# Feed-forward by seven products: weights prepared two parts ahead, sums made one unit earlier, another product order, and one halved down block instead of two

## The chip, the cores and the metric

The kernel runs on one core of a Trainium2 chip. The metric is the time of one execution on the device in microseconds (us). The kernel before has a median of 1240.38 us over three timed runs (1239.95 to 1240.4). One further execution was taken with the hardware profiler; all durations below are from it.

The core has five engines that run side by side, each in its own order: TensorE (PE: matmuls, with PEld for the loading of their weights), VectorE (DVE), ScalarE (ACT), GpSimd (POOL) and SyncE (SP, which only issues transfers). They wait for one another through semaphores. Transfers (DMA) are issued by SP, POOL and ACT, each with a queue of its own.

## The reference

One layer of an encoder: 512 tokens, 1024 features, float32. Two token mixers (a gated DeltaNet with 8 heads and a banded attention with 16) are merged; then come a cross-attention into 256 memory tokens, a SwiGLU feed-forward network (FFN) with 2816 hidden features, and a final norm. What the change touches, with its surroundings:

```python
oa = _gated_deltanet(qa, ka, va, alpha, beta, a_log[l], dt_bias[l])
oa = rmsnorm(oa, head_norm[l]) * jax.nn.silu(za.reshape(b, s, A_HEADS, A_DV))
...
x = x + _memory_xattn(rmsnorm(x, norm_xattn[l]), rmsnorm(mem, norm_mem[l]),
                      w_mq[l], w_mkv[l], w_mo[l])
gate, up = _split_cols(rmsnorm(x, norm_ffn[l]) @ w_gate_up[l], (D_FF, D_FF))
x = x + (jax.nn.silu(gate) * up) @ w_down[l]
return rmsnorm(x, norm_final)
```

## The kernel before

**Products.** Activations lie with features on the 128 partitions and tokens along the row. A float32 product is made from halves: every operand is split into a high part (`whi`, `fh`, `guh`, written by ScalarE, L111) and a low part (`wlo`, `fl`, `gul`, the rest, written by VectorE, L113), and three matmuls (high x high, high x low, low x high) are summed in PSUM. So each weight is loaded by SP into a `raw` buffer, split, and used; `raw`, `whi` and `wlo` have three buffers each.

**Order of the work.** PE runs in the order of the program text. `drive` (L173) takes the steps of the present products; after each step `advance` (L168) moves every generator in the list `pending` one step on, so `wait(n)` holds something back by n steps. A `side` generator advances once a step. ACT, DVE, POOL and SP run in an order that a scheduler of the compiler chooses; where a tile needs a buffer, the pool's ring decides whose last reader it waits for.

**Last head of the DeltaNet.** `head_out` (L494) computes `zs`, the normed and gated output of a head; `oa_tile` (L537) transposes it on PE (`oaT`, L542), one head later in general. For the last head there is no later one: it waits 6 steps and is transposed between the tiles `nat` of the next product. A `nat` tile is 24 matmuls, two k to a step.

**FFN, blocks 0 to 2.** The 22 blocks of 128 hidden features have one gate and one up product each. For the first three, `ffn_gemm` makes them plainly, each 24 matmuls of 512 tokens, on the activations before the norm; `ffn_after` (L1101) empties the gate's PSUM into `fa` (L1104: times the row factor of the norm, silu, times the factor again) and then the up product into `gu` (L1108). PSUM for these has three slots (`PM`), so the third up block takes the slot of the second gate block. Tiles `fa` have tag "c", with three buffers.

**Sums of the activations.** Beside these blocks `ffn_sums` (L1114) normalises the activations (`xn`, two tiles in each of four rounds) and makes from their quarters (feature half by token half) the seven operands of a fast 2x2 product: three plain (11, 21, 22) and four sums (T1 to T4, `ft`), each split into `fh` and `fl`, 256 tokens wide.

**FFN, units 3 to 21.** A `unit` (L1166) makes both gate and up of one block from seven products instead of eight. Its weights are the quarters of `w_g[j]` and `w_u[j]`: three plain ones (a11, a12, a22) and four sums s1 to s4 (`fs`). s1 and s3 are summed by the transfer itself: a load by SP (L1172), then an accumulating transfer by POOL (L1173, L1174). s2 and s4 are added on VectorE (L1196, L1197). `quarter` (L1156) splits one into high and low, and is called as an argument of `product` (12 matmuls of 256 tokens, L1186 to L1188), so right ahead of its use. The order is 11, T2, T1, T3, 21, T4, 22. After each product a few operations add its PSUM into `fe`, `fU`, `fW`, `fcc`; the last one (L1219) makes the block's `gu`. s1, s3 and s4 share tag "ti" with four buffers, s2 has "th".

**Down product.** `gu_split` splits a `gu` block into `guh` and `gul`. Blocks 0 to 4 are split beside units 9 to 13; of the rest, three are split ahead of the first down block and the others beside it. Of the 8 output blocks of 128 features, 0 to 5 run whole (`series`: 66 matmuls of 512 tokens, then the residual sum and the sum of squares `acc`, by POOL). Blocks 6 and 7 run in two halves of 256 tokens (`wd_last`), so that `final` (L1267), the norm of a half, can begin on the first half under the second. Its sum of squares takes `acc` and one `sq` for each halved block.

Of the kernel before, what the change touches and what calls it, by code (L numbers as in the profile page):

```python
# [40 lines left out]
def hybrid_block(  # L41
# [452 lines left out]
    def head_out(hd):  # L494

        on, ss = kT[hd], SM("ss", 4)
        pu_, pq = PD("oU"), PS("oS")
        for n in range(NT):
            c = slice(n * P, (n + 1) * P)
            nc.tensor.matmul(out=pu_[:, c], lhsT=PT[hd][:, c], rhs=vs[hd][:, c], start=True, stop=True)  # L500
        yield
        for n in range(1, NT):
            c = slice(n * P, (n + 1) * P)
            nc.tensor.matmul(out=pq[:, c], lhsT=qT[hd][:, c], rhs=S[hd, n - 1], start=True, stop=True)
        yield
# [12 lines left out]
        f = SM("f", 4)  # L518
        nc.vector.scalar_tensor_tensor(out=f, in0=ss, scalar=1.0 / P, in1=fe[hd], op0=ALU.mult, op1=ALU.add)
        nc.gpsimd.tensor_tensor(out=f, in0=f, in1=mhalf, op=ALU.pow)  # L520
        yield from wait(2)
        z = zs[hd // 2]
        zc = slice((hd % 2) * P, (hd % 2) * P + P)
        for n in range(NT):
            nc.vector.scalar_tensor_tensor(out=z[:, n, zc], in0=on[:, n * P : (n + 1) * P], scalar=f[:, n : n + 1],
                                           in1=z[:, n, zc], op0=ALU.mult, op1=ALU.mult)
# [587 lines left out]
    def ffn_sums():  # L1114

        for n in NB:
            B[n] = []
        for i in range(4):
            x = []
            for k in (i, i + 4):  # L1120
                t = TMP("xn", "th")
                nc.vector.scalar_tensor_tensor(out=t, in0=x3[k], scalar=gain(C_FFN, k), in1=stat["row3"],
                                               op0=ALU.mult, op1=ALU.mult)
# [39 lines left out]
        split(hi, lo, src)  # L1163
        return hi, lo

    def unit(j):  # L1166
        raws = [wp.tile([P, KD, P], F32, tag="raw", bufs=3, name=nm("raw")) for _ in range(2)]
        a11, a12, a22 = raws[0][:, 0:4, :], raws[0][:, 4:8, :], raws[1][:, 0:4, :]
        s1, s3, s4, s2 = (TMP("fs", t).rearrange("p (k f) -> p k f", k=4) for t in ("ti", "ti", "ti", "th"))
        nc.sync.dma_start(out=raws[0], in_=w_g[j])  # L1170
        for s in (s1, s3):
            nc.sync.dma_start(out=s, in_=w_u[j][:, 0:4, :])  # L1172
        nc.gpsimd.dma_start(out=s1, in_=w_u[j][:, 4:8, :], accum_op=ALU.add)  # L1173
        nc.gpsimd.dma_start(out=s3, in_=w_g[j][:, 0:4, :], accum_op=ALU.add)  # L1174
        nc.sync.dma_start(out=a22, in_=w_u[j][:, 4:8, :])
        e, U = TMP("fe", "c"), TMP("fU", "c")
        W, sg, cc = TMP("fW", "c"), TMP("fg", "th"), TMP("fcc", "th")
        tt = nc.vector.tensor_tensor
        rot = [PM, PD, PS, PM, PD, PM, PD]

        def product(ps, w, act):
# [8 lines left out]

        def bank(i):
            return rot[i]("fp")
        p1 = bank(0)
        yield from product(p1, quarter(a11), "11")
        nc.scalar.activation(e[:, lh], p1[:, lh], AF.Copy)
        tt(out=s2, in0=s1, in1=a11, op=ALU.add)  # L1196
        tt(out=s4, in0=a12, in1=s2, op=ALU.add)  # L1197
# [3 lines left out]
        p = bank(2)  # L1201
        yield from product(p, quarter(s1), "T1")
        tt(out=W[:, lh], in0=U[:, lh], in1=p[:, lh], op=ALU.add)
        q = bank(3)
        yield from product(q, quarter(s3), "T3")
        tt(out=U[:, rh], in0=U[:, lh], in1=q[:, lh], op=ALU.add)
        tt(out=cc[:, rh], in0=W[:, lh], in1=q[:, lh], op=ALU.add)
        p = bank(4)
        yield from product(p, quarter(a12), "21")
        tt(out=e[:, lh], in0=e[:, lh], in1=p[:, lh], op=ALU.add)  # L1210
        nc.scalar.activation(sg[:, lh], e[:, lh], AF.Silu)
        p = bank(5)
        yield from product(p, quarter(a22), "T4")
        tt(out=cc[:, lh], in0=U[:, rh], in1=p[:, lh], op=ALU.add)
        p = bank(6)
        yield from product(p, quarter(s4), "22")
        tt(out=W[:, lh], in0=W[:, lh], in1=p[:, lh], op=ALU.add)
        nc.scalar.activation(sg[:, rh], W[:, lh], AF.Silu)
# [48 lines left out]
    def final(tok, sq):  # L1267
        yield from wait(6)
        ps = [PS("r4") for _ in range(2)]
        for i, q in enumerate([acc4[:, tok]] + sq):  # L1270
            for tt in range(2):
                nc.tensor.matmul(out=ps[tt][:, 0:1], lhsT=q[:, tt * P : tt * P + P], rhs=ones[:, 0:1],  # L1272
                                 start=(i == 0), stop=(i == 2))
        var, rs = SM("r4", 2), SM("r4", 2)
        for tt in range(2):
            nc.vector.tensor_scalar(out=var[:, tt : tt + 1], in0=ps[tt][:, 0:1], scalar1=1.0 / D, scalar2=EPS,  # L1276
# [9 lines left out]
            nc.vector.tensor_tensor(out=x, in0=x, in1=pr[:, :H].unsqueeze(1).to_broadcast([P, 2, H]), op=ALU.mult)  # L1286
            (nc.scalar if i in (0, 2) else nc.sync).dma_start(out=outT[i][:, :, tok], in_=x)

    wd = series(w_d, dps, gu, wd_after, range(KD - 2), kt=KF, pieces=PIECES)
    side = gu_splits(range(5, KF))  # L1290
    for _ in range(3):
        next(side)
    drive(wd[0], side=side)
    drive(*wd[1:])
    for hf in range(2):
        tok, sq = slice(hf * H, hf * H + H), []
        drive(*[(wd_last(j, tok, PM("wd"), sq), None) for j in (KD - 2, KD - 1)])
        pending.append(final(tok, sq))
    flush()

# [71 lines left out]
```

## Time and profile before

| What | Value |
|---|---|
| median of three timed runs | 1240.38 us (1239.95 to 1240.4) |
| profiled execution | 1234.58 us, its span 1232.9 us |
| granted clock, mean over the execution | 0.989 |
| ACT, DVE, POOL busy | 47%, 62%, 12% |
| data moved | 149.28 MB, mean 121 GB/s |
| units 3 to 21 | 886.78 to 1094.51 us |
| down blocks 0 to 5 | 1094.51 to 1189.02 us |

The timed runs and the profiled execution are different executions; times inside the kernel are from the latter, and they are us from the start of the span. A row of a group or of the timeline reads "output<-inputs", with the program's names. What stands in brackets behind a row is the idle time of the engine just before it and what ended that. The granted clock is the share of TensorE's full clock that the chip's throttle let through.

### The profile page before, as it was taken

What the parts mean: (1) busy time and instruction counts of PE and PEld (TensorE: products, weight loads), DVE (VectorE), ACT (ScalarE), POOL (GpSimd) and SP (SyncE); (2) the same over time, 40 slices, a digit from 0 to 9 for tenths busy, and PEclk for the clock granted to TensorE, in tenths of its full rate; (3) what the DMA queues carried; (4) which work ended last, traced back from release to release, by engine and by line L of the source; (5) the groups of instructions that cost most, each with busy time, mean ns of one, the idle gap of its engine ahead of it and who ended that gap; (6) DMA issues with size and microseconds to landing.
All of it is one profiled execution on the core that took longest, in us unless ns stands there. A gap on an engine that the chain in (4) does not pass through costs nothing. (4 is left out here: it accounts for less than half of the span.)

```text
span 1232.9 us, 19731 instructions
## 1 busy us (share of the span) xinstructions
PE 1204.3 (98%) x7571; PEld 1052.7 (85%) x7571; DVE 764.0 (62%) x1564; ACT 584.9 (47%) x1207; POOL 144.8 (12%) x143
## 2 busy tenths in 40 slices
PE   9999999999999999999999999999899989999997
PEld 8778888899988887777888998888699989988887
DVE  5967882355633488775464654554978878882233
ACT  7573234465741477665333443443544545462232
POOL 0022230310110000000122200013011111100000
PEclk9999999999999999999999999999989999999998
DMA  7253343212433432223324462123167666743343
GB/s 278 87 177 102 123 119 98 94 43 70 149 122 106 162 103 90 90 86 111 108 98 145 135 210 83 52 69 103 49 159 184 168 159 172 190 118 94 94 124 116
DMA packets 73054, 149.28 MB, mean 121 GB/s; under 512 B 19041, under 2 KB 27649, under 8 KB 72961
## 3 DMA queue, kind: packets, MB, share of 16 engines
q1 hardware_dynamic: 66400, 137.02, 34.4%
q0 software_dynamic: 5472, 9.96, 5.1%
q8 instruction: 59, 0.97, 0.3%
q10 hardware_dynamic: 1088, 1.05, 0.2%
q14 instruction: 35, 0.28, 0.1%
HBM read 140.13 MB, written 7.88 MB: 120 GB/s over the span
## 5 line engine op out<-in xcount | busy, mean ns | idle before, releaser
L111 ACT ACTIVATE whi<-raw 128x1024 fp32r<-128x1024 f32 (+4 forms) x224 | 206.4, 926 | 310.5 <-PE g L138 80.9
L113 DVE TENSOR_TENSOR wlo<-raw,whi 128x1024 fp32r<-128x1024 f32 (+4 forms) x210 | 228.5, 1092 | 156.3 <-ACT whi L111 155.1
L1188 PE MATMUL fp<-fh,wlo 128*128 128x256 f32 x532 | 153.2, 288 | 3.7 <-DVE wlo L113 3.7
L1186 PE MATMUL fp<-fh,whi 128*128 128x256 f32 x532 | 152.8, 287 | 3.7 <-ACT whi L111 3.4
L1187 PE MATMUL fp<-fl,whi 128*128 128x256 f32 x532 | 152.6, 287 | 2.0 <-DVE fl L113 2.0
L1188 PEld LDWEIGHTS fp<-fh,wlo 128*128 128x128 f32 x532 | 104.1, 196 | 4.8 <-DVE wlo L113 4.8
L1186 PEld LDWEIGHTS fp<-fh,whi 128*128 128x128 f32 x532 | 104.1, 196 | 4.4 <-ACT whi L111 3.9
L1187 PEld LDWEIGHTS fp<-fl,whi 128*128 128x128 f32 x532 | 104.2, 196 | 2.3 <-DVE fl L113 2.2
L111 ACT ACTIVATE whi<-fs 128x512 fp32r<-128x512 f32 x76 | 46.4, 626 | 62.4 <-PE fp L1187 46.7
L203 POOL TENSOR_TENSOR acc<-acc,sq 128x512 f32<-128x512 f32 x19 | 31.6, 1665 | 265.2 <-issue 161.3
L162 PE MATMUL nat<-whi,hh 128*128 128x256 f32 x192 | 58.5, 304 | 0.4 <-DVE conv L391 0.4
L164 PE MATMUL nat<-wlo,hh 128*128 128x256 f32 x192 | 55.0, 286 | 0.0
L163 PE MATMUL nat<-whi,hl 128*128 128x256 f32 x192 | 54.9, 286 | 0.0
L113 DVE TENSOR_TENSOR wlo<-fs,whi 128x512 fp32r<-128x512 f32 x76 | 51.1, 686 | 6.0 <-ACT whi L111 5.4
L138 PE MATMUL g<-gul,whi 128*128 128x512 f32 x132 | 52.5, 398 | 1.9 <-DVE gul L113 1.9
L139 PE MATMUL g<-guh,wlo 128*128 128x512 f32 x132 | 52.2, 396 | 0.0
L137 PE MATMUL g<-guh,whi 128*128 128x512 f32 x132 | 52.0, 394 | 0.0
L799 ACT ACTIVATE P<-P,mx 128x128 f32<-128x128 f32 (+1 forms) x64 | 35.8, 560 | 28.7 <-DVE mx L797 28.5
L113 POOL TENSOR_TENSOR wlo<-raw,whi 128x1024 fp32r<-128x1024 f32 x14 | 34.0, 2430 | 106.3 <-ACT whi L111 106.3
L162 PEld LDWEIGHTS nat<-whi,hh 128*128 128x128 f32 x192 | 37.5, 195 | 1.4 <-issue 0.6
L1173 POOL DMA_DIRECT2D fs<-in_w_u x19 | 16.7, 876 | 185.5 <-DMA fs<-in_w_u 69.4
L163 PEld LDWEIGHTS nat<-whi,hl 128*128 128x128 f32 x192 | 37.4, 195 | 0.0
(416 smaller groups left out, 3327.7 us busy)
## 6 DMA issues: line engine op xcount, KB each, us to landing
raw<-in_w_g SPq DMA_DIRECT2D x22, 512.0 KB, 5.6
raw<-in_w_d SPq DMA_DIRECT2D x20, 512.0 KB, 3.6
fs<-in_w_u SPq DMA_DIRECT2D x38, 256.0 KB, 3.8
fs<-in_w_u POOLq DMA_DIRECT2D x19, 256.0 KB, 3.9
fs<-in_w_g POOLq DMA_DIRECT2D x19, 256.0 KB, 6.3
raw<-in_w_u SPq DMA_DIRECT2D x19, 256.0 KB, 4.0
raw<-in_wk SPq DMA_DIRECT2D x8, 512.0 KB, 3.8
raw<-in_wga SPq DMA_DIRECT2D x8, 512.0 KB, 3.6
```

The costliest lines, as they stand in the source:

```text
L111: nc.scalar.activation(hi, src, AF.Copy, scale=1.0 if scale is None else scale)
L113: (eng or nc.vector).tensor_tensor(out=lo, in0=src, in1=hi.bitcast(F32), op=ALU.subtract)
L137: nc.tensor.matmul(out=ps[:, :w], lhsT=hi[:, k - a, :], rhs=xh[:, n], start=first, stop=False)
L138: nc.tensor.matmul(out=ps[:, :w], lhsT=hi[:, k - a, :], rhs=xl[:, n], start=False, stop=False)
L139: nc.tensor.matmul(out=ps[:, :w], lhsT=lo[:, k - a, :], rhs=xh[:, n], start=False, stop=last)
L162: nc.tensor.matmul(out=o, lhsT=xh[:, tok], rhs=hi[:, kw, :], start=(k == 0), stop=False)
L163: nc.tensor.matmul(out=o, lhsT=xl[:, tok], rhs=hi[:, kw, :], start=False, stop=False)
L164: nc.tensor.matmul(out=o, lhsT=xh[:, tok], rhs=lo[:, kw, :], start=False, stop=(k == KD - 1))
L799: nc.scalar.activation(pr, pr, AF.Exp, scale=-1.0, bias=mx, accum_out=rs[:, t : t + 1])
L1186: nc.tensor.matmul(out=o, lhsT=hi[:, k, :], rhs=xh, start=k == 0, stop=False)
L1187: nc.tensor.matmul(out=o, lhsT=hi[:, k, :], rhs=xl, start=False, stop=False)
L1188: nc.tensor.matmul(out=o, lhsT=lo[:, k, :], rhs=xh, start=False, stop=k == 3)
```

## The change

- The last head's `oaT` waits 12 steps instead of 6.
- `ffn_sums` takes all its `fh` and `fl` buffers at the start, two operands to a tile in the pairs (11, 21), (22, T1), (T2, T3), (T4, unused). Its `xn` tiles move from tag "th" to tag "c", which they share with `fa`.
- In the units, `loads(j)` issues the transfers and the two VectorE sums of unit j. It is called within the stream of parts of the unit before, at its sixth part. `take` keeps the stream up to two parts ahead of the product that runs. s4 moves from "ti" to "th".
- The order of the products is 11, 21, 22, T2, T1, T3, T4, and the operations that empty PSUM follow it, with the same number of them.
- Blocks 5 to 12 of `gu` are split beside the last unit, 13 to 21 beside the first down block.
- Only down block 7 runs in halves; block 6 runs whole, and the final norm has one `sq` for each half.

```diff
         if hd == AH - 1:
-            yield from wait(6)
+            yield from wait(12)
             yield from oa_tile(hd)
...
+        tiles = {}
+        for at in range(4):
+            for i in range(4):
+                tiles[i, at] = [G("a" if at < 2 else "b", n, F32R) for n in ("fh", "fl")]
         for i in range(4):
             x = []
             for k in (i, i + 4):
-                t = TMP("xn", "th")
+                t = TMP("xn", "c")
...
-            his = [G("a" if i < 2 else "b", "fh", F32R) for _ in range(4)]
-            los = [G("a" if i < 2 else "b", "fl", F32R) for _ in range(4)]
             for at, n in enumerate(NB):
                 o = lh if at % 2 == 0 else rh
-                B[n].append((his[at // 2][:, o], los[at // 2][:, o]))
+                B[n].append([t[:, o] for t in tiles[i, at // 2]])
...
-    def unit(j):
+    def loads(j):
+
         raws = [wp.tile([P, KD, P], F32, tag="raw", bufs=3, name=nm("raw")) for _ in range(2)]
         a11, a12, a22 = raws[0][:, 0:4, :], raws[0][:, 4:8, :], raws[1][:, 0:4, :]
-        s1, s3, s4, s2 = (TMP("fs", t).rearrange("p (k f) -> p k f", k=4) for t in ("ti", "ti", "ti", "th"))
-        nc.sync.dma_start(out=raws[0], in_=w_g[j])
+        s1, s3, s2, s4 = (TMP("fs", t).rearrange("p (k f) -> p k f", k=4) for t in ("ti", "ti", "th", "th"))
         for s in (s1, s3):
             nc.sync.dma_start(out=s, in_=w_u[j][:, 0:4, :])
+        nc.sync.dma_start(out=raws[0], in_=w_g[j])
         nc.gpsimd.dma_start(out=s1, in_=w_u[j][:, 4:8, :], accum_op=ALU.add)
         nc.gpsimd.dma_start(out=s3, in_=w_g[j][:, 0:4, :], accum_op=ALU.add)
         nc.sync.dma_start(out=a22, in_=w_u[j][:, 4:8, :])
+        tt(out=s2, in0=s1, in1=a11, op=ALU.add)
+        tt(out=s4, in0=a12, in1=s2, op=ALU.add)
+        return a11, a12, s4, s2, s1, s3, a22
+
+    def quarters():
+        srcs = loads(NCL)
+        for j in range(NCL, KF):
+            now = srcs
+            for n in range(7):
+                if n == 5 and j + 1 < KF:
+                    srcs = loads(j + 1)
+                yield quarter(now[n])
+
+    stream, ready = quarters(), []
+
+    def take():
+        while len(ready) < 3:
+            ready.append(next(stream, None))
+        return ready.pop(0)
...
-        yield from product(p1, quarter(a11), "11")
+        yield from product(p, take(), "11")
...
-        yield from product(p, quarter(s2), "T2")
+        yield from product(p, take(), "21")
...
+        if j == KF - 2:
+            pending.append(seq(wait(10), gu_splits(range(5, 9)), wait(8), gu_splits(range(9, 13))))
...
-                                 start=(i == 0), stop=(i == 2))
+                                 start=(i == 0), stop=(i == len(sq)))
...
-    wd = series(w_d, dps, gu, wd_after, range(KD - 2), kt=KF, pieces=PIECES)
-    side = gu_splits(range(5, KF))
-    for _ in range(3):
-        next(side)
+    wd = series(w_d, dps, gu, wd_after, range(KD - 1), kt=KF, pieces=PIECES)
+    side = gu_splits(range(13, KF))
...
-        drive(*[(wd_last(j, tok, PM("wd"), sq), None) for j in (KD - 2, KD - 1)])
+        drive(*[(wd_last(j, tok, PM("wd"), sq), None) for j in (KD - 1,)])
```

Three places show how instructions move (numbers behind a name tell its buffers apart, and they differ between the two programs).

On PE at the end of the DeltaNet, before the change, the transposes of the last head follow a finished `nat` tile and stand ahead of the next:

```order
L162 MATMUL nat_3991<-whi_3790,hh_546 128x256
L163 MATMUL nat_3991<-whi_3790,hl_547 128x256
L164 MATMUL nat_3991<-wlo_3791,hh_546 128x256
L542 MATMUL oaT_4016<-ident,zs_284 128x128 x4
L162 MATMUL nat_4040<-whi_4030,hh_434 128x256
```

On PE at the same place after the change, the tile that came behind `oaT` (there `nat_4040`, here `nat_4031`) is finished first:

```order
L162 MATMUL nat_4031<-whi_4027,hh_546 128x256
L163 MATMUL nat_4031<-whi_4027,hl_547 128x256
L164 MATMUL nat_4031<-wlo_4028,hh_546 128x256
L542 MATMUL oaT_4056<-ident,zs_284 128x128 x4
L162 MATMUL nat_4068<-whi_4021,hh_434 128x256
```

So 24 matmuls moved ahead of the four transposes.

On DVE in the first FFN blocks, before the change, the second gate block's `fa` (`fa_8846`, from PSUM `ff_8678`) stands between the first and the second round's sums, 19 rows behind the first `xn`:

```order
L113 TENSOR_TENSOR fl_8646<-xn_8636,fh_8642 128x256
L113 TENSOR_TENSOR fl_8648<-ft_8650,fh_8644 128x256
L113 TENSOR_TENSOR fl_8708<-xn_8688,fh_8704 128x256
L1104 TENSOR_TENSOR fa_8846<-ff_8678,rrow_8624 128x512
L1122 SCALAR_TENSOR_TENSOR xn_8697<-x_2_6726,cst,rrow_8624 128x512
L1139 TENSOR_TENSOR ft_8712<-xn_8688 128x256
L113 TENSOR_TENSOR wlo_8883<-raw_8880,whi_8882 128x1024
```

On DVE after the change, the same `fa_8846` stands in the fourth round, 52 rows behind the first `xn`:

```order
L1149 SCALAR_TENSOR_TENSOR ft_8778<-ft_8777,xn_8765 128x256
L113 TENSOR_TENSOR fl_8652<-ft_8778,fh_8651 128x256
L113 TENSOR_TENSOR fl_8652<-ft_8777,fh_8651 128x256
L113 TENSOR_TENSOR fl_8646<-ft_8819,fh_8645 128x256
L1142 SCALAR_TENSOR_TENSOR ft_8819<-ft_8819,xn_8814 128x256
L1145 TENSOR_TENSOR ft_8820<-xn_8814,xn_8809 128x256
L1104 TENSOR_TENSOR fa_8846<-ff_8702,rrow_8624 128x512
L113 TENSOR_TENSOR fl_8638<-xn_8814,fh_8637 128x256
```

So 33 more instructions stand ahead of it, all of them sums, splits of sums, or weight splits; its buffer is one that an `xn` held (`xn_8765`, last read by the first row shown).

On SP's queue while the cross-attention's `mem_v` product runs, as one piece of the difference (`raw` from `in_w_mv` are its weights, `fs` from `in_w_u` are the loads for s1 and s3 of the units):

```order
 L120 DMA raw_7500<-in_w_mv 128x1024
-L1172 DMA fs_8918<-in_w_u 128x512
-L1172 DMA fs_8919<-in_w_u 128x512
+L1176 DMA fs_8924<-in_w_u 128x512
+L1176 DMA fs_8925<-in_w_u 128x512
+L1176 DMA fs_8996<-in_w_u 128x512
 L120 DMA raw_7506<-in_w_mv 128x1024
+L1176 DMA fs_8997<-in_w_u 128x512
 L120 DMA raw_7568<-in_w_mv 128x1024
```

The two loads of unit 3 were there already; the two of unit 4 (`fs_8996`, `fs_8997`) join them, one ahead of `raw_7506` and one ahead of `raw_7568`.

More of the change, by code (lines that the diff above doesn't have):

```diff
@@ L1192, in bank @@
             return rot[i]("fp")
[L1193 to L1199 removed]
+        p = bank(0)
+        yield from product(p, take(), "11")
+        nc.scalar.activation(e[:, lh], p[:, lh], AF.Copy)
+        p = bank(1)
+        yield from product(p, take(), "21")
+        tt(out=sg[:, lh], in0=e[:, lh], in1=p[:, lh], op=ALU.add)
+        nc.scalar.activation(sg[:, lh], sg[:, lh], AF.Silu)
+        q = bank(2)
+        yield from product(q, take(), "22")
+        p = bank(3)
+        yield from product(p, take(), "T2")
         tt(out=U[:, lh], in0=e[:, lh], in1=p[:, lh], op=ALU.add)
[L1201 to L1202 removed]
+        p = bank(4)
+        yield from product(p, take(), "T1")
         tt(out=W[:, lh], in0=U[:, lh], in1=p[:, lh], op=ALU.add)
[L1204 to L1211, printed above, removed]
[L1212 to L1213 removed]
+        tt(out=sg[:, rh], in0=W[:, lh], in1=q[:, lh], op=ALU.add)
+        nc.scalar.activation(sg[:, rh], sg[:, rh], AF.Silu)
+        p = bank(5)
+        yield from product(p, take(), "T3")
+        tt(out=U[:, rh], in0=U[:, lh], in1=p[:, lh], op=ALU.add)
+        tt(out=cc[:, rh], in0=W[:, lh], in1=p[:, lh], op=ALU.add)
+        p = bank(6)
+        yield from product(p, take(), "T4")
         tt(out=cc[:, lh], in0=U[:, rh], in1=p[:, lh], op=ALU.add)
[L1215 to L1218, printed above, removed]
         nc.vector.scalar_tensor_tensor(out=gu_tile(), in0=cc, scalar=-1.0, in1=sg, op0=ALU.mult, op1=ALU.mult)
```

3 lines of the change are left out of this document (2 added, 1 removed).

## The prediction

> **What bounds the kernel now.** I read the page's head first, for the busy shares.
>
> ```profile
> span 1232.9 us, 19731 instructions
> ...
> PE 1204.3 (98%) x7571; PEld 1052.7 (85%) x7571; DVE 764.0 (62%) x1564; ACT 584.9 (47%) x1207; POOL 144.8 (12%) x143
> ```
>
> TensorE (PE) is the bound. No matmul is saved in bulk, so a gain can only be PE's idle time and the slow matmuls behind it. Where that is, the waits of PE (us in total, times, longest) and then the windows by stage say (us, busy time and count of PE, PEld, DVE, ACT and POOL, granted clock, DMA share, GB/s).
>
> ```profile
> PE fp L1188 <- DVE wlo L113: 3.7, 4, 1.9
> PE fp L1186 <- ACT whi L111: 3.4, 2, 1.9
> PE oaT L542 <- DVE zs L525: 2.2, 1, 2.2
> PE fp L1187 <- DVE fl L113: 2.0, 1, 2.0
> PE g L138 <- DVE gul L113: 1.9, 3, 1.4
> ```
>
> ```profile
> 347.46:351.38 3.92, 1.73 (x12) 1.24 (x11) 3.02 (x6) 1.72 (x3) 1.94 (x2) 1.00 0.41 120
> 351.38:354.79 3.41, 3.41 (x19) 3.41 (x18) 1.07 (x2) 0.30 (x1) 0.00 (x0) 0.50 0.61 213
> 886.78:906.20 19.42, 14.20 (x85) 13.21 (x84) 14.84 (x34) 8.23 (x18) 2.69 (x3) 0.74 0.45 115
> 906.20:916.28 10.08, 10.08 (x86) 10.08 (x85) 8.31 (x17) 4.51 (x10) 0.86 (x1) 1.00 0.69 173
> 998.10:1013.45 15.35, 11.97 (x87) 11.56 (x85) 11.06 (x22) 7.12 (x14) 2.59 (x3) 0.89 0.60 137
> 1094.51:1113.88 19.37, 17.52 (x68) 13.29 (x67) 13.42 (x20) 9.21 (x17) 0.00 (x0) 0.91 0.38 109
> 1113.88:1128.91 15.03, 15.03 (x68) 12.39 (x66) 4.10 (x4) 4.36 (x6) 0.00 (x0) 1.00 0.34 94
> ```
>
> An undisturbed unit takes 10.08 us, an undisturbed down block 15.03. The first unit (at 886.78), unit 13 (at 998.10) and the first down block (at 1094.51) are longer, and in each the clock is below 1. A wait is thus paid twice: once idle, once in a stretch of half clock, of which the row at 351.38 is one of 3.41 us.
>
> **The change part by part.**
>
> *Last oaT, 24 matmuls later.* Here is PE around it, and VectorE's zs that it waits for.
>
> ```profile
> 347.46 0.28 PE L164 MATMUL nat<-wlo,hh 128*128 128x256 f32 x1
> 349.93 1.02 PE L542 MATMUL oaT<-ident,zs 128*128 128x128 f32 x4 [2.19 <-DVE zs L525]
> ...
> 351.59 0.41 PE L162 MATMUL nat<-whi,hh 128*128 128x256 f32 x1
> 351.80 0.41 PE L163 MATMUL nat<-whi,hl 128*128 128x256 f32 x1
> ```
>
> ```profile
> 349.43 1.14 DVE L525 SCALAR_TENSOR_TENSOR zs<-kT,f,zs 128x128 f32<-128x128 f32 x4 [0.90 <-POOL f L520]
> ```
>
> At full clock a 256-wide matmul takes 10.08/84 = 0.12 us; at half clock 0.21 (351.59 to 351.80). The half-clock stretch loses 3.41 x (1 - 0.12/0.21) = 1.5 us. With the wait: 2.2 + 1.5 = 3.7. A whole tile of 24 matmuls now stands ahead and covers 24 x 0.12 = 2.88 us: oaT's turn comes at 347.58 + 2.88 = 350.46, zs ends at 350.57. At most 0.1 stays, too short for a half-clock stretch by the row on 1.5 us below. Gain **3.7**.
>
> *First unit (19.42 - 10.08 = 9.34 us over).* Unit 3 now has its first weights split early and all four rounds of sums made beforehand, so its own stalls go. But fa and xn now share the three buffers of tag "c", and VectorE does the sums first: fa_8846, which empties the second gate block's PSUM, stood 19 rows behind the first xn and now stands 52 behind. Its durations, start to start, are in these rows:
>
> ```profile
> 861.68 1.41 DVE L1122 SCALAR_TENSOR_TENSOR xn<-x,cst,rrow 128x512 f32<-128x512 f32 x2 [1.56 <-ACT rrow L236]
> 863.01 0.68 DVE L1104 TENSOR_TENSOR fa<-ff,rrow 128x512 f32<-128x512 f32 x1
> 863.61 0.41 DVE L1139 TENSOR_TENSOR ft<-xn 128x256 f32<-128x256 f32 x1
> 863.94 0.42 DVE L113 TENSOR_TENSOR fl<-xn,fh 128x256 fp32r<-128x256 f32 x1
> ...
> 866.79 1.22 DVE L113 TENSOR_TENSOR wlo<-raw,whi 128x1024 fp32r<-128x1024 f32 x1
> 867.93 0.42 DVE L1147 SCALAR_TENSOR_TENSOR ft<-ft,xn 128x256 f32<-128x256 f32 x1
> ```
>
> ```profile
> 881.16 0.39 PE L137 MATMUL ff<-xh,whi 128*128 128x512 f32 x1
> ```
>
> One xn takes (863.01 - 861.68)/2 = 0.665 us, a 512-wide fa 0.60 (863.01 to 863.61; gu and the 512-wide wlo are taken as that), a 256-wide ft or fl 0.335 (863.61 to 863.94), a 1024-wide wlo 1.14 (866.79 to 867.93). The 52 rows are 8 xn, 37 ft and fl, 3 of fa and gu, 2 wide and 2 narrow wlo: 5.3 + 12.4 + 1.8 + 2.3 + 1.2 = 23.0 us. So fa_8846 starts at 861.68 + 23.0 = 884.7 and ends at 885.3. The third up block takes that PSUM slot and in the trace starts at 881.16: a **new wait of 4.2 us**, and about 1.6 for one half-clock stretch behind it (the 1.5 above, with room for where it falls). Queued behind that waiting matmul is all the rest of PE's work. The next slot is emptied by a gu 14 rows later: seven of 0.335 and seven of 0.60, so 885.3 + 6.6 = 891.9, while PE ends the up block at 885.3 + 5.6 + 1.6 = 892.5: not late. Unit 3 then starts 5.8 later, with bounds of 4.2 (no half clock) and 9.3 (as much as now). Gain 9.34 - 5.8 = **3.5**.
>
> [...]
>
> *Later units.* Here are the eighteen other units in one window, ScalarE's wait in them, and their transfers (KB each, median us to landing).
>
> ```profile
> 906.20:1094.51 188.31, 184.10 (x1515) 183.08 (x1513) 160.00 (x312) 96.01 (x189) 28.50 (x33) 0.99 0.67 170
> ```
>
> ```profile
> ACT whi L111 <- DMA fs<-in_w_g: 7.4, 6, 2.6
> ```
>
> ```profile
> fs<-in_w_u SPq DMA_DIRECT2D x32, 256.0 KB, 3.2
> ...
> fs<-in_w_g POOLq DMA_DIRECT2D x17, 256.0 KB, 6.3
> fs<-in_w_u POOLq DMA_DIRECT2D x16, 256.0 KB, 3.9
> ```
>
> They lose 188.31 - 18 x 10.08 = **6.9**, of which unit 13 alone 15.35 - 10.08 = 5.3. ScalarE waits six times for the accumulated sum s3, whose buffers (tag "ti", three of four taken by each unit) come free only in the same unit. Now s1 and s3 alone use that tag, so two units' worth fit, and loads are made a unit ahead. In series: load 3.2, accumulates 3.9 and 6.3, two sums of 0.6, together 14.6 us. There are some 11 us until the first part with a sum is due and three products of 10.08/7 = 1.44 in the weight buffers, 15.3 in all. It fits, if closely, even in series; in truth the accumulates overlap. VectorE's work per unit (8.31 of 10.08) stays. I take the whole 6.9.
>
> *First down block.* 19.37 - 15.03 = 4.3 over, from gul splits made beside it. Eight of them now lie in the last unit, nine remain; the k-th is needed 15.03/22 = 0.68 us after the one before, and VectorE makes one in 0.60. Gain **4.3** (2 if VectorE is late in the last unit: eight at 0.60 are 4.8 us on top of its 8.3, less two wlo and two sums that the last unit has no successor for, 2.4; 0.6 us over, which the first k in the queue have in hand).
>
> *One down block whole instead of halved.* A half takes this:
>
> ```profile
> 1189.02:1196.92 7.90, 7.90 (x67) 7.90 (x66) 3.83 (x4) 4.29 (x5) 1.29 (x1) 1.00 0.53 158
> ```
>
> 2 x 7.90 - 15.03 = 0.8, and four fewer one-column matmuls, about 0.2. The squares go through POOL's acc instead, hidden under the next half. Gain **1.0**. The tail is unchanged.
>
> *Two transfers moved into mem_v.* Unit 4's two fs loads now stand on SP's queue between raws of mem_v, and two more accumulates on POOL's.
>
> ```profile
> 720.00:725.00 5.00, 5.00 (x44) 5.00 (x43) 2.84 (x4) 1.53 (x2) 0.00 (x0) 1.00 0.95 258
> ```
>
> ```profile
> 726.20 1.23 DVE L113 TENSOR_TENSOR wlo<-raw,whi 128x1024 fp32r<-128x1024 f32 x1 [1.14 <-ACT whi L111]
> ```
>
> ```profile
> 729.86 0.28 PE L162 MATMUL nat<-whi,mg 128*128 128x256 f32 x1
> ```
>
> There the transfer engines are 0.95 busy already. 512 KB more at 258 GB/s lands 2.0 us later; the wlo that ends at 727.43 is used from 729.86 on, 2.4 us in hand. Between 0 and 1.5 us with the accumulates on top; I take **0.3**.
>
> **Sum.** 3.7 + 3.5 + 6.9 + 4.3 + 1.0 - 0.3 = 19.1 us, from a profiled execution of 1234.58 (1.7 above its span): 1215.5. The median of the timed runs is 5.8 higher, at 1240.38, so the time is **1221** on that scale.
>
> **The rivals.**
>
> *Entry dearer.* Two or three half-clock stretches behind the new wait, or VectorE pausing for ScalarE's fh within those 52 rows, so that unit 3 starts about as late as it now ends its stalls: 9.3 instead of 5.8, sum 15.6, time 1225. For it: the clock of 0.74 over the whole of the present first unit. Against: unit 13 at a clock of 0.89 was slow for 2 x 0.11 x 15.35 = 3.4 us, one stretch, behind waits of the same sum.
>
> *Entry cheaper.* The wait passes without half clock, as this one did:
>
> ```profile
> PE ka L137 <- DVE conv L391: 1.5, 1, 1.5
> ```
>
> ```profile
> 84.90:88.30 3.40, 3.10 (x14) 2.58 (x15) 2.65 (x13) 3.16 (x4) 1.01 (x1) 1.00 0.42 146
> ```
>
> That gives 1.6 back: 1219.5. Against: it was 1.5 us, and 2.19 already brought half clock. [...]
>
> *It does not do what it says.* The weights are not really ahead: the sums still land late, the 6.9 stay, and mem_v stalls by its 1.5: sum 11.0, time 1229. For it: the engines that move data are 0.69 busy in an undisturbed unit already.
>
> *Slower.* If both accumulates take 6.3 us in series, the chain is 3.2 + 12.6 + 1.2 = 17.0 against 15.3; past that point every unit waits. 18 units x 1.7 = 31 us lost, time 1240.4 - 19.1 + 31 = 1252. Against: the accumulates overlap, and the median of one is 3.9.
>
> **How the numbers follow.** The forecast has 0.54 (its own range 1217 to 1224), entry dearer 0.15, the late sums 0.13, entry cheaper 0.09, slower 0.06, and 0.03 for several losses together that end near the old time. The range 1215 to 1231 takes in all but the last two. About 0.2% (2.5 us) is what a measurement of this kernel can tell from no change: faster 0.91, same 0.03, slower 0.06.
>
> **What would show it.** Of the changed profile: oaT's wait gone and the clock 1.00 behind it; a wait of PE's third up block on VectorE of about 4 us near 881, followed by a clock of 0.5; every unit at 10.08; no wait on gul; a first down block of 15.0. I am wrong if fa is not late, if units run above 10.1 with ScalarE waiting on fs, or if mem_v's nat stalls near 730.

## The result and the profile after

The changed kernel has a median of 1219.03 us over four runs (1217.89 to 1221.12), the kernel before 1240.26 us over four. The ratio is 0.9831, with a 95% interval of 0.9814 to 0.9848. The prediction was 1221 us, with a range of 1215 to 1231. The profiled execution of the changed kernel took 1218.92 us, and this is its head, in the columns of the page.

```profile
span 1217.2 us, 19571 instructions
...
PE 1195.3 (98%) x7497; PEld 1044.3 (86%) x7497; DVE 762.4 (63%) x1560; ACT 580.9 (48%) x1202; POOL 146.1 (12%) x144
```

The spans differ by only 15.7 us, though the medians differ by 21.2. The table says why: it cuts both profiled executions at the same instructions of PE.

| Stage, from the first ... to the first ... | before, us | after, us | gain | predicted |
|---|---|---|---|---|
| start to x product of the DeltaNet | 192.64 | 192.71 | -0.07 | - |
| x product to oaT (not changed) | 120.59 | 124.91 | -4.32 | - |
| oaT to mem_v | 399.35 | 395.10 | 4.25 | 3.7 |
| mem_v to gate block 0 | 138.70 | 139.11 | -0.41 | -0.3 |
| gate block 0 to unit 4 | 54.92 | 51.44 | 3.48 | 3.5 |
| unit 4 to the down product | 188.31 | 181.44 | 6.87 | 6.9 |
| first down block | 19.37 | 15.03 | 4.34 | 4.3 |
| the other down blocks | 108.38 | 107.17 | 1.21 | 1.0 |
| end of the matmuls to the end | 10.61 | 10.29 | 0.32 | 0 |

The stages from oaT on gain 20.06 us. The second row is the same program in both, and it was 4.3 longer in this execution; its length changes from one execution to the next, which the runs below show. So the two profiled executions understate the change. The medians agree with the stages: the interval of their ratio is 18.9 to 23.1 us and holds the 20.06.

These are the longest waits of PE in the changed kernel, and then the windows that answer to those shown before (us; busy time and count of PE, PEld, DVE, ACT, POOL; granted clock; DMA share; GB/s).

```profile
PE ff L137 <- DVE fa L1104: 4.1, 1, 4.1
PE ka L137 <- DVE conv L391: 1.8, 1, 1.8
PE x L619 <- issue: 1.5, 1, 1.5
```

```profile
881.70:885.97 4.27, 0.16 (x1) 0.03 (x1) 4.27 (x12) 2.25 (x7) 0.00 (x0) 1.00 0.00 0
885.97:893.20 7.23, 7.23 (x25) 5.74 (x25) 7.01 (x15) 2.91 (x6) 0.00 (x0) 0.76 0.11 39
893.20:903.27 10.07, 10.07 (x85) 10.07 (x84) 8.41 (x16) 5.41 (x11) 1.83 (x2) 1.00 0.59 148
903.27:1084.71 181.44, 181.44 (x1514) 181.44 (x1513) 162.48 (x312) 96.28 (x191) 27.61 (x32) 1.00 0.70 174
1084.71:1099.74 15.03, 15.03 (x68) 12.40 (x67) 12.58 (x19) 7.76 (x13) 0.00 (x0) 1.00 0.45 130
```

The waits of `fp`, `oaT` and `g` that headed the list before are gone (one of `nat` on `wlo`, up to 0.8 us, stays further down). Nineteen units take 191.51 us in all, 19 x 10.08: PE is busy in every part of them, at a clock of 1.00. One new wait heads the list: the third up block waits 4.1 us for VectorE's `fa`, and behind it the clock falls to 0.76 over the block, 7.23 us instead of 5.62.

### The profile page after: what moved, and what is told of

It reads as the page before. It is cut to its first block, busy times and chain, and to the rows that moved or that the text cites. A ratio compares the mean times of both kernels' runs of the same rounds, so it can differ in the third digit from the quotient of the medians.

```text
span 1217.2 us, 19571 instructions
## 1 busy us (share of the span) xinstructions
PE 1195.3 (98%) x7497; PEld 1044.3 (86%) x7497; DVE 762.4 (63%) x1560; ACT 580.9 (48%) x1202; POOL 146.1 (12%) x144
## 4 chain that ended last, share of the span: by engine, by line
PE 81%; DVE 1%; issue 1%; DMA 1%; ACT 0%; POOLq 0%; POOL 0%; DVEq 0%; ACTq 0%
PE g L137 6%; PE g L138 6%; PE g L139 6%; PE fp L1211 5%; PE fp L1213 5%; PE fp L1212 5%; PE nat L162 2%; PE nat L164 2%; PE nat L163 2%; PE pt L815 2%; PE ob L823 2%; PE kb L137 1%; PE gb L137 1%; PE qa L137 1%; PE qb L137 1%; PE mq L137 1%
## 5 line engine op out<-in xcount | busy, mean ns | idle before, releaser
L111 ACT ACTIVATE whi<-raw 128x1024 fp32r<-128x1024 f32 (+4 forms) x221 | 202.8, 926 | 311.0 <-PE g L138 91.3
L113 DVE TENSOR_TENSOR wlo<-raw,whi 128x1024 fp32r<-128x1024 f32 (+4 forms) x207 | 224.8, 1092 | 151.1 <-ACT whi L111 150.4
L1213 PE MATMUL fp<-fh,wlo 128*128 128x256 f32 x532 | 150.7, 283 | 0.0
L139 PE MATMUL g<-guh,wlo 128*128 128x512 f32 x154 | 60.1, 390 | 0.0
L138 PE MATMUL g<-gul,whi 128*128 128x512 f32 x154 | 60.1, 390 | 0.0
L137 PE MATMUL g<-guh,whi 128*128 128x512 f32 x154 | 60.1, 390 | 0.0
```

The source lines that it names most:

```text
L111: nc.scalar.activation(hi, src, AF.Copy, scale=1.0 if scale is None else scale)
L113: (eng or nc.vector).tensor_tensor(out=lo, in0=src, in1=hi.bitcast(F32), op=ALU.subtract)
L137: nc.tensor.matmul(out=ps[:, :w], lhsT=hi[:, k - a, :], rhs=xh[:, n], start=first, stop=False)
L138: nc.tensor.matmul(out=ps[:, :w], lhsT=hi[:, k - a, :], rhs=xl[:, n], start=False, stop=False)
L139: nc.tensor.matmul(out=ps[:, :w], lhsT=lo[:, k - a, :], rhs=xh[:, n], start=False, stop=last)
L1213: nc.tensor.matmul(out=o, lhsT=lo[:, k, :], rhs=xh, start=False, stop=k == 3)
```

## The experiments

All are the changed kernel with one thing altered, except where the text says otherwise. Since the stage from the x product to oaT is so uneven, the time of a run has an interval of half a per cent or more; what is compared is the stage that the edit touches. As long as its program is the same and PE does not wait in it, a stage repeats within 0.1 us from execution to execution. Where PE waits it repeats less well: the last up block behind the 4.1 us wait took 7.23 us at a mean clock of 0.76 in the changed kernel and 8.14 us at 0.67 in oaT6, and mem_v's stage took from 138.70 to 139.69 us.

### The same kernel again

> The changed kernel once more, as the measure for the two others, and to see which of its stages repeat. Theory (what is before the last head's oaT is the same program in all kernels of this study, and its length changes from execution to execution): the stage from the first x product to the first oaT differs by some us from the 124.9 of the first profile, all the later stages repeat within 0.6. Rival (the change itself lengthened that stage, 120.6 before): 124.9 again.

The median was 1220.97 us, the ratio to the kernel before 0.9836 (0.9781 to 0.989). From oaT on, no stage differs from the first profile by more than 0.5 us, and that one is mem_v, 138.70 here. The stage from the x product to oaT took 137.73 us, which refutes the rival: the same instructions took 120.6, 124.9 and 137.7. This is its row, with the stretch behind its one long wait:

```profile
193.52:331.25 137.73, 135.30 (x1093) 121.70 (x1094) 57.68 (x139) 62.31 (x192) 15.32 (x7) 0.86 0.18 59
```

```profile
204.00:232.00 28.00, 28.00 (x190) 25.44 (x179) 4.71 (x7) 4.94 (x9) 0.00 (x0) 0.50 0.06 20
```

The busy time is the clock's, not a wait's: 28 us at half clock with PE never idle.

### oaT back at its old place

```diff
-            yield from wait(12)
+            yield from wait(6)
```

> The changed kernel, with only the last head's oaT put back to 6 steps. Theory (the wait for zs and the half clock behind it were on the path, 4.1 us: 2.2 idle, 1.5 half clock, some between the transposes): 4.1 above the changed kernel's 1219.0, so 1223. Rival (something later would have absorbed it): 1219.

The median was 1224.56 us, the ratio 0.989 (0.9859 to 0.9922). The wait is back, and its stage (first oaT to mem_v) is 399.37 us, against 395.10 with the edit and 399.35 before:

```profile
PE oaT L542 <- DVE zs L525: 2.2, 1, 2.2
```

So the 4.3 us are this edit's alone, and nothing later absorbs them.

### The splits of gu back beside the first down block

```diff
-        if j == KF - 2:
-            pending.append(seq(wait(10), gu_splits(range(5, 9)), wait(8), gu_splits(range(9, 13))))
...
-    side = gu_splits(range(13, KF))
+    side = gu_splits(range(5, KF))
+    for _ in range(3):
+        next(side)
```

> The changed kernel, with the splits of gu 5 to 12 taken out of the last unit again (three ahead of the first down block, the others beside it). Theory (the first down block was short of gul): 4.3 more, 1223. Rival (in the changed kernel the last unit leaves VectorE time enough that the splits are early anyway): less than 1 more, 1219 to 1220.

The median was 1221.31 us, the ratio 0.9869 (0.9839 to 0.9899). The window of the first down block:

```profile
1088.67:1103.71 15.04, 15.04 (x69) 12.40 (x67) 12.58 (x19) 7.76 (x13) 0.00 (x0) 1.00 0.45 130
```

15.04 against 15.03. But this edit moved nothing: VectorE and ScalarE ran the same instructions in the same order as in the changed kernel, and the same six low halves `gul` start in the last unit. These are VectorE's rows of the changed kernel, where the down product begins at 1084.71, and then of this run, where it begins at 1088.67:

```profile
1077.27 0.69 DVE L113 TENSOR_TENSOR gul<-gu,guh 128x512 fp32r<-128x512 f32 x1
1078.20 0.69 DVE L113 TENSOR_TENSOR gul<-gu,guh 128x512 fp32r<-128x512 f32 x1
1079.41 1.29 DVE L113 TENSOR_TENSOR gul<-gu,guh 128x512 fp32r<-128x512 f32 x2
1083.09 1.29 DVE L113 TENSOR_TENSOR gul<-gu,guh 128x512 fp32r<-128x512 f32 x2
```

```profile
1081.23 0.69 DVE L113 TENSOR_TENSOR gul<-gu,guh 128x512 fp32r<-128x512 f32 x1
1082.17 0.68 DVE L113 TENSOR_TENSOR gul<-gu,guh 128x512 fp32r<-128x512 f32 x1
1083.38 1.28 DVE L113 TENSOR_TENSOR gul<-gu,guh 128x512 fp32r<-128x512 f32 x2
1087.05 1.29 DVE L113 TENSOR_TENSOR gul<-gu,guh 128x512 fp32r<-128x512 f32 x2
```

So the place of the calls in the text does not set where the splits run. Whether the block would wait without early splits is not tested by this run: it speaks neither for the theory nor for the rival. In the kernel before, four low halves start in the last unit, the first of them 4.66 us ahead of the down product instead of 7.44.

### The products in their old order

The products run 11, T2, T1, T3, 21, T4, 22, with the evacuations of before.

> The changed kernel with the products and the operations behind them in the old order (11, T2, T1, T3, 21, T4, 22); loads a unit ahead and all the rest stay changed. Theory (with the loads ahead the order is free, and at the entry VectorE's work ends about 0.6 later): 1219 to 1220. Rival (that the plain halves lead is needed for the entry, since T2 and s2 come last out of VectorE): 3 to 5 us in unit 3, 1222 to 1224.

The median was 1222.32 us, the ratio 0.9894 (0.9833 to 0.9955). The entry (gate block 0 to unit 4) took 53.30 us, 1.9 more: the wait for `fa` was 4.7 instead of 4.1 us, and the other 1.25 us are a longer half clock behind it (8.48 instead of 7.23 us for the last up block). The units took 181.44 as with the new order. But the first down block took 18.97, and PE waits there for `gul` again:

```profile
1083.93:1102.90 18.97, 16.28 (x68) 12.01 (x67) 13.42 (x20) 9.05 (x16) 0.00 (x0) 1.00 0.36 105
```

```profile
PE g L138 <- DVE gul L113: 2.7, 4, 1.4
```

Theory and rival had both left this out. It happened though eight splits are called in the last unit; only four low halves start there, as in the kernel before. The splits of gu 5 to 12 are written into tag "a", those of 13 to 20 into "b", and both tags hold the operands of the seven products. In the old order 21 and 22 are the fifth and the last product and hold "a" to the end; in the new order 11 and 21 are over after two. The order of VectorE's instructions bears it out: with the old order the splits run 13, 14, 5, 15, 6, 16, ..., and 12 comes last of all; with the new one they run 5 to 10, then 13, 11, 14, 12. So do the times. These are the first `guh` of the last unit, in the old order (unit from 1073.85) and then in the changed kernel (unit from 1074.63):

```profile
1078.61 1.16 ACT L111 ACTIVATE guh<-gu 128x512 fp32r<-128x512 f32 x2 [1.17 <-PE fp L1212]
```

```profile
1076.61 1.15 ACT L111 ACTIVATE guh<-gu 128x512 fp32r<-128x512 f32 x2
```

A product takes 1.44 us and reads its four operand tiles one after the other, 0.36 us each. In the old order the first split, that of 13, needs the first tile of T2 and T3; T3 is the fourth product and is through with that tile after 3 x 1.44 + 0.36 = 4.68 us. ScalarE waits for PE and starts 4.76 us into the unit. In the new order the first split, that of 5, needs the first tile of 11 and 21, free after 1.44 + 0.36 = 1.80 us, and starts at 1.98.

### The operand tiles as before

```diff
-        tiles = {}
-        for at in range(4):
-            for i in range(4):
-                tiles[i, at] = [G("a" if at < 2 else "b", n, F32R) for n in ("fh", "fl")]
...
+            his = [G("a" if i < 2 else "b", "fh", F32R) for _ in range(4)]
+            los = [G("a" if i < 2 else "b", "fl", F32R) for _ in range(4)]
...
-                B[n].append([t[:, o] for t in tiles[i, at // 2]])
+                B[n].append((his[at // 2][:, o], los[at // 2][:, o]))
```

> The changed kernel with the operand tiles allocated as before, round by round (rounds 0 and 1 in tag a), products in the new order. In the run with the old order the first down block was 19.0 and waited for gul, though eight splits lay in the last unit. Theory (the order decides which operands are read last, so which buffers come free for the splits): with the new order 15.0 to 15.5 also in the old tiles. Rival (the pairs of operands in a tile are needed for it): 18 to 19. The rest unchanged, entry within 1.

The median was 1222.34 us, the ratio 0.9857 (0.9789 to 0.9926). The first down block took 15.79 us, with one wait of 0.4 for `gul`:

```profile
1097.06:1112.85 15.79, 15.35 (x68) 12.34 (x67) 12.58 (x20) 7.88 (x13) 0.00 (x0) 1.00 0.43 123
```

So most of the gain is there with the old tiles too, and the pairs of operands in a tile give the last 0.8, which is a little more than the theory allowed them. Against the 19.37 of the kernel before the new order with old tiles gains 3.6, though these two differ in more than the order. The entry took 52.26 us, 0.8 more, with a wait of 5.0 us at the same place, ended here by ScalarE's `whi`.

### Loads and sums in the unit's own place

`loads(j)` is called at unit j's first part, and `take` fetches only the part that is due. Either edit alone leaves the instructions of SP, VectorE and ScalarE in the order of the changed kernel, so only both together are an experiment: the "two parts ahead" and the "unit ahead" are two ways to say one thing.

```diff
-        srcs = loads(NCL)
         for j in range(NCL, KF):
-            now = srcs
+            now = loads(j)
             for n in range(7):
-                if n == 5 and j + 1 < KF:
-                    srcs = loads(j + 1)
                 yield quarter(now[n])
...
-        while len(ready) < 3:
+        while len(ready) < 1:
```

> The changed kernel with loads(j) called at unit j's own first part and the stream not kept ahead, so that transfers and the two sums stand in the unit's own place again; buffers and order of products stay changed. Theory (the buffers of ti and the order of the products do the work): units 4 to 21 within 2 us of 181.4, first down block within 1 of 15.0, so 1219 to 1222. Rival (loading in the unit before is what cures): about 5 us lost in the units and 2 to 4 in the first down block, 1226 to 1228.

The median was 1250.68 us, the ratio 1.0123 (1.0066 to 1.0179): slower than the kernel before. The units, and the waits that fill them:

```profile
902.32:1115.27 212.95, 197.21 (x1515) 193.27 (x1514) 162.77 (x313) 98.53 (x191) 27.79 (x32) 0.94 0.61 148
```

```profile
PE fp L1210 <- DVE wlo L113: 11.0, 10, 2.2
PE fp L1208 <- ACT whi L111: 4.7, 9, 0.5
```

31.5 us more than 181.44, six times what the rival priced for the units, and the theory fell. The new order needs s4, the sum of sums, for its third product instead of its last. With the loads in the unit's own place about every second unit waits for it. The first down block is 15.03 all the same, which agrees with the two runs above: it does not hang on the place of the loads.

### The buffers alone

This is the kernel before, with s4 in tag "th":

```diff
-        s1, s3, s4, s2 = (TMP("fs", t).rearrange("p (k f) -> p k f", k=4) for t in ("ti", "ti", "ti", "th"))
+        s1, s3, s4, s2 = (TMP("fs", t).rearrange("p (k f) -> p k f", k=4) for t in ("ti", "ti", "th", "th"))
```

> The kernel before, with one edit: s4 has tag th instead of ti, so that ti's four buffers hold s1 and s3 of two units. Theory (the buffers alone let the accumulated sums come in time): the 6.9 us of the later units go, 1240.3 - 6.9 = 1233, and the entry into unit 3 stays as it is. Rival (loading in the unit before is what does it): 1240.

The median was 1230.77 us, the ratio 0.9959 (0.9926 to 0.9992). Its profiled execution had a long second stage (137.43 us), so its stages are read, not its span:

```profile
920.73:1103.66 182.93, 181.95 (x1514) 181.54 (x1513) 159.94 (x312) 95.11 (x189) 27.85 (x32) 1.00 0.66 170
1103.66:1121.42 17.76, 15.91 (x69) 12.16 (x67) 13.43 (x20) 9.21 (x17) 0.00 (x0) 1.00 0.42 118
```

The units went from 188.31 to 182.93: 5.4 of the 6.9 us come from the buffers alone, with the old order, where s4 is due last. The run with the old order and the loads ahead had 181.44, so loading ahead is worth the other 1.5 there. The entry took 54.01, 0.9 less than before. The first down block has the same waits on `gul` as before (1.9 us in all) and is 1.6 us shorter, at a clock of 1.00 instead of 0.91.

### A buffer of its own for fa

```diff
-        a = TMP("fa", "c")
+        a = TMP("fa", "fa", 1)
```

> The changed kernel, with one buffer of its own for fa instead of tag c. Theory A (the shared buffers are the whole cause of the 4.1 us wait of the third up block): wait and half clock go, 5.9 us less, 1213. Theory B (VectorE has more work than time in this stretch, the shared buffer only decides which product waits): the up block no longer waits, but the third product of unit 3 waits for the low half of s4, which by the durations ends at 893.9 and is due at 890.5: 3.4 us and 1.5 of half clock, so only 1.0 less, 1218.

The median was 1218.84 us, the ratio 0.9881 (0.9815 to 0.9946). The third up block no longer waits, but unit 3 does. Here are PE's longest waits and the stretch from gate block 0 to unit 4, which took 51.44 us with the shared buffers:

```profile
PE fp L1213 <- DVE wlo L113: 1.9, 1, 1.9
PE fp L1211 <- ACT whi L111: 1.2, 1, 1.2
```

```profile
852.01:902.71 50.70, 47.59 (x246) 40.58 (x244) 43.04 (x89) 26.39 (x54) 4.62 (x4) 0.97 0.25 73
```

0.7 us instead of 5.9: theory A fell, and theory B foretold 1.0. The low half of s4 ends at 894.1, foretold for 893.9. VectorE has more work than time in this stretch, and the buffer only decided who waits for it.

### Work of the entry moved to POOL

fa's own buffer; the weights' low halves of the last gate and up block and fa's second multiplication on POOL. (The expectation names the up block alone; the edit holds for both.)

```diff
-        yield from block_steps(store[j], w[j], x3g)
+        yield from block_steps(store[j], w[j], x3g, eng=nc.gpsimd if j == 2 else None)
...
-        a = TMP("fa", "c")
+        a = TMP("fa", "fa", 1)
...
-        nc.vector.tensor_tensor(out=a, in0=a, in1=row3, op=ALU.mult)
+        nc.gpsimd.tensor_tensor(out=a, in0=a, in1=row3, op=ALU.mult)
```

> The changed kernel with three edits at the entry into the units: fa has one buffer of its own, the last up block's weight low halves are made by POOL, and fa's second multiplication is made by POOL. Theory B of fa_own (VectorE has too much to do there): by the row durations fa of the second gate block is out 5 us before it is due and the low half of s4 1 us before, so no wait is left from the first gate block to unit 4: 5.9 less than the changed kernel, 1213. Rival (POOL's slower work, 2.4 us for a wide low half and about 1.7 for the multiplication, becomes the wait, or unit 3 waits for ScalarE): 1216 to 1219.

The median was 1223.08 us, the ratio 0.9889 (0.9841 to 0.9938), and the stretch took 54.49 us, 3 more instead of 6 less; the rival was too cheap as well. These are POOL's and VectorE's rows there:

```profile
866.98 3.46 POOL L113 TENSOR_TENSOR wlo<-raw,whi 128x1024 fp32r<-128x1024 f32 x1 [6.99 <-ACT whi L111]
870.39 1.75 POOL L1106 TENSOR_TENSOR fa<-fa,rrow 128x512 f32<-128x512 f32 x1
...
893.39 3.48 POOL L1106 TENSOR_TENSOR fa<-fa,rrow 128x512 f32<-128x512 f32 x1 [5.91 <-ACT fa L1105]
```

```profile
867.75 0.41 DVE L113 TENSOR_TENSOR fl<-xn,fh 128x256 fp32r<-128x256 f32 x1
868.09 2.90 DVE L1126 SCALAR_TENSOR_TENSOR xn<-x,cst,rrow 128x512 f32<-128x512 f32 x1
870.91 1.51 DVE L113 TENSOR_TENSOR fl<-ft,fh 128x256 fp32r<-128x256 f32 x1
...
875.03 2.88 DVE L1126 SCALAR_TENSOR_TENSOR xn<-x,cst,rrow 128x512 f32<-128x512 f32 x1
...
878.50 0.68 DVE L1108 TENSOR_TENSOR gu<-ff,fa 128x512 f32<-128x512 f32 x1
...
879.44 0.74 DVE L1126 SCALAR_TENSOR_TENSOR xn<-x,cst,rrow 128x512 f32<-128x512 f32 x1
```

Two `xn` that meet POOL's low halves take 2.9 us instead of 0.74. What POOL took over cost VectorE more than it saved: its busy time in the stretch is 45.49 us, against 43.04 with fa's own buffer alone. A gate block then waited 2.1 us for `gu`, which VectorE reached at 878.50, behind the slow `xn`; POOL's multiplication for it had ended at 872.14.

### Work of the entry put off

fa's own buffer again; the splits of T3 and T4 are made in unit 3, right ahead of their products, and their sums wait in free buffers of another pool; unit 3's products take other PSUM banks.

```diff
-        rot = [PM, PD, PS, PM, PD, PM, PD]
+        rot = [PM, PD, PS, PS, PD, PD, PD] if j == NCL else [PM, PD, PS, PM, PD, PM, PD]
...
         p = bank(4)
+        if j == NCL:
+            late_splits("T3", lh)
         yield from product(p, take(), "T1")
```

> The changed kernel with three edits at the entry: fa has a buffer of its own; the splits of T3 and T4 are made only in unit 3, ahead of their products (their sums wait in four free buffers of pool v); unit 3 puts three products into other PSUM banks, so that none of them waits for the last gate and up blocks. Theory (VectorE has too much to do ahead of the third product, and 5.4 us of it can wait): by the row durations the low half of s4 is out at 890.0, due at 890.5; from the first gate block to unit 4 46.5 us instead of 51.4, so about 5 less than the changed kernel, 1214. Rival (ScalarE, or evacuations that now come late, hold it): 1 to 2 less.

The median was 1215.93 us, the ratio 0.9808 (0.9746 to 0.9871). The stretch, and the units behind it:

```profile
852.95:898.66 45.71, 45.71 (x246) 39.05 (x245) 39.35 (x82) 25.71 (x53) 4.65 (x4) 1.00 0.23 72
898.66:1081.32 182.66, 181.66 (x1515) 181.49 (x1514) 165.06 (x319) 96.90 (x192) 27.64 (x32) 1.00 0.70 175
```

PE never idles from gate block 0 to unit 4, and the clock stays at 1.00: 5.7 us less. The three edits were not tried one by one. One wait of 1.0 us is left in unit 4, for the evacuation of a PSUM bank. The last kernel gives that product another bank:

```diff
+        elif j == NCL + 1:
+            rot[1] = PM
```

> entry_defer with one product of unit 4 put into another PSUM bank, which by entry_defer's trace comes free 0.3 us before it is due, where the old one came 1.0 us late. Theory (that bank was what its one wait hung on): units 4 to 21 back at 181.4 us from 182.7, all waits gone from the first gate block to the last down block, 1.2 less than entry_defer. Rival (VectorE, full up to there, is late with the next thing instead): the wait moves to a later product of unit 4 or 5, no gain.

The median was 1213.04 us, the ratio 0.9811 (0.9762 to 0.9859). The only wait of PE from mem_v to the last down block is one of 0.2 us, and units 4 to 21 take 181.84 us: 0.8 of the 1.2 us came. By its stages it is 5.7 us ahead of the changed kernel in the entry and 0.4 behind in the units. The timed runs alone do not separate the two: the intervals of their ratios overlap (0.9762 to 0.9859 and 0.9814 to 0.9848).

## Why the prediction was right, and where it was not

**What bounds the kernel.** PE, by its waits and the half clock behind them: right. No matmul was saved in bulk, and the gain is in the waits that went.

**oaT.** Right, and mis-sized: 3.7 predicted, 4.25 measured. The term took the wait that the profile names, 2.19 us. These rows of the kernel before and then of the changed one show the rest:

```profile
350.71 0.36 PE L162 MATMUL nat<-whi,hh 128*128 128x256 f32 x1
```

```profile
354.74 0.28 PE L164 MATMUL nat<-wlo,hh 128*128 128x256 f32 x1
354.86 0.60 PE L542 MATMUL oaT<-ident,zs 128*128 128x128 f32 x4
355.21 0.37 PE L162 MATMUL nat<-whi,hh 128*128 128x256 f32 x1
```

From the last `nat` matmul to the next one PE took 350.71 - 347.46 = 3.25 us before and 355.21 - 354.74 = 0.47 after, 2.8 less: the four transposes had also followed the four pieces of `zs` one by one. With 1.5 for the half clock that is the 4.25, within 0.05.

**Entry.** Right in mechanism and size: 3.48 against 3.5, with the new wait at its place. The wait was counted from 52 instructions of VectorE, priced at 23.0 us from the first `xn` to `fa`; in the changed kernel `fa` starts at 885.13, 22.98 us behind the first `xn` at 862.15. The wait was to be 4.2 us long and was 4.1:

```profile
885.97 0.47 PE L137 MATMUL ff<-xh,whi 128*128 128x512 f32 x1 [4.11 <-DVE fa L1104]
```

The half clock behind it was to cost 1.6 and cost 7.23 - 5.62 = 1.6 here. In other runs that kept a wait at this place it cost 1.5 (oldpair, behind 5.0 us), 2.5 (oaT6, behind 4.1) and 2.9 (oldorder, behind 4.7), so that 1.6 is partly luck: the second stretch of the dearer rival nearly came in some runs, though never its 9.3 us. What the prediction did not say, and fa_own showed, is that a wait at the third product stands behind this one; the two share one cause, VectorE's work.

**Later units.** Right: 6.87 against 6.9. The buffers of "ti", which the prediction named, give 5.4 of it in the old order, and loading ahead the rest. The loading a unit ahead was taken as a second reason of like kind; in the new order it is the condition, worth 31.5 us. The rival on the slower side (a chain longer than its window) did not occur, but loadsown shows that a slower result was near: with s4 due third, load, accumulate and the two sums must be done before the unit's third product. How much of its 31.5 us is the accumulates is not shown.

**First down block.** The size was right (4.34 against 4.3), and the step that gave the reason was half right: "Eight of them now lie in the last unit". Six low halves start there, against four before, and eleven remain instead of nine; PE waits for none of them. But it is not the place of the calls that put them there: calling them later moved none, and in the old order only four start there in spite of the calls. What did it is the order of the products, which frees the buffers of tag "a" early in the last unit (18.97 us against 15.03), and the pairs of operands in a tile (15.79 against 15.03). There is some luck in the size: 1.6 of the 19.37 us before were half clock, and ti_only with the same waits had none of it.

**Halving, mem_v.** 1.21 against 1.0; no run takes the halving alone, so how the 1.21 divides is not shown, nor what gave the 0.32 at the end, which the sum put at nothing. That mem_v has -0.41 against -0.3 is luck: its wait came in some executions of the same kernel and not in others (139.11 and 138.70 us for its stage in the two of the changed kernel, 138.70 before).

**The scale.** The sum was made against an execution 5.8 us below the median. The uneven stage that no edit touches explains that the two profiled executions differ by less than the medians; the clock in it differs (0.97 and 0.86 in the two executions of the changed kernel, 1.00 before), and what makes the clock differ is open.

## What to carry to other kernels

When a wait goes, ask which engine's work stood behind it: here the buffer, the bank and the third product were three places to wait for one overfull VectorE, and putting off work that was not yet due gave nearly all of the gain there (5.7 us). An order of products decides not only when operands are needed but when their buffers come free for the next phase (a first down block of 18.97 us against 15.03); calling the next phase's work earlier in the text does nothing where a buffer holds it or a scheduler places it (15.03 us against 15.04). So look in the trace whether an edit moved an instruction before reading its time. Between executions that vary by more than the effect, compare the stage that the edit touches, cut at the same instructions.

## What the runs showed of the hardware

The clock stayed at half for 28 us in a stretch in which PE was busy without a gap (204 to 232 us in the second execution of the changed kernel); in its first execution the clock was 0.57 from 201.4 to 204.8 us and 1.00 from 205 to 232. The matmuls' ends in a profile are modelled, so "without a gap" is what the profile shows. What released the clock is not known.

Work moved to POOL slowed VectorE: while POOL made a 1024-wide low half (3.46 us, where the kernel before has a mean of 2.43 on POOL), a 512-wide product of three operands on VectorE took 2.90 us instead of 0.74, and a 256-wide low half beside POOL's multiplication took 1.51 us instead of 0.41. Not every row beside POOL's work is slower: the low half at 867.75, of the same form, kept its 0.41. POOL's three multiplications, of one form, took 1.75, 4.21 and 3.48 us; beside the start of the second, at 883.28, VectorE's rows at 883.37 and 883.71 kept their 0.41. What decides which of the two engines pays is not shown.

Behind the 4.1 us wait of the third up block the clock fell, to a mean of 0.76 over the block in the changed kernel and 0.67 in oaT6. With oaT at its old place it fell behind 2.2 us, to 0.50 over 3.41 us in the kernel before. Behind 1.0 us in unit 4 it stayed at 1.00 over the units in entry_defer. The three waits for `gul` in the first down block, 1.9 us in all, had a clock of 0.91 in the kernel before and 1.00 in ti_only. So the same waits came with half clock and without, and how long a wait must be to lower the clock is not shown.
